# Strassen weight sums by accumulating DMA, and a third of K through Strassen, in a decoder trunk's shared K/V projection

## The chip, the cores and the metric

One Trainium2 chip, one core. The metric is the device time of one launch in microseconds (us), the median of several runs. TensorE is called PE here, VectorE DVE, ScalarE ACT, GpSimd POOL and SyncE SP, as the profile does.

## The reference

A two-layer decoder trunk on 256 tokens and 256 memory tokens of width 2048, in float32. Layer A is retention with a memory branch. After it, K and V for three groups of dilated attention are projected from the normalized residual stream; layer B uses them. The part that the change is about:

```python
def shared_kv(x, g, w_kv):
    B, S, _ = x.shape
    parts = split_cols(rmsnorm(x, g) @ w_kv, [DIL_W] * (2 * len(DIL_CONFIG)))
    return [t.reshape(B, S, DIL_HEADS, DIL_DH) for t in parts]
```

`w_kv` is 2048 x 12288: K1, V1, K2, V2, K3, V3 of 2048 columns each (K3 is called K's third group below). The memory's K and V of each layer are `rmsnorm(mem) @ w_mem_kv`.

## The kernel before

Every large product runs on PE in fp32r. A float32 operand is split into a high and a low part, and three of the four partial products are kept. A weight tile of 128 x 1024 floats (512 KB) comes from HBM into one of 6 buffers `raw`, on SP's queue. ACT casts it to `wh` (line 97), DVE computes `wl = raw - wh` (line 98). There are 5 pairs of `wh`/`wl`; `high_priority` lets these splits run ahead of PE, and a `raw` buffer is free when its last reader is done.

Two ways of multiplying matter here:

- `dense_cols` (line 306) computes a chunk of 512 columns, transposed: for each of 8 weight tiles, 8 pairs of a 512-column matmul (line 315, high part of the weight times high and low part of the input side by side) and a 256-column matmul (line 317): 64 pairs a chunk. K is made this way, 12 chunks. Its results have the columns on the partitions, which is what the attention wants of K.
- `strassen` (line 343) computes 1024 columns with 7 products of half-size blocks instead of 8, rows (tokens) on the partitions. One "pair" (of chunks) is 28 pieces, each ended by a `yield`: 4 steps d of four pieces (first phase: b0, b1, b2, b3), then 4 steps of three. A piece, which the text calls a product, is one split weight tile and 6 matmuls of 512 columns (lines 371 to 373). In the first phase a step loads w11, w12, w22 and needs three sums: s1 = w11 + w12, w12 + w22 (in place), s2 = s1 + w22 (line 361); in the second phase one load, w21, and s2 + w21. V is made this way, 6 pairs. The inputs of four of the products are differences of blocks of y, made by `combine`.

The generators of the Strassen pairs stand in the queue `woven`; `dense_cols` calls `weave(n)` to run n of their pieces after each of its weight tiles. Other small work stands in `pending`, one piece per `step()`. The framework's scheduler then fixes the order of each engine's queue; each queue runs strictly in that order. POOL's queue holds little else than the DMAs to and from DRAM: `spill` (line 778) puts a result into DRAM when it has been evicted from PSUM, `fetch` brings it back.

The order of stages: memory K and V of layer A, layer A, its output projection, memory K and V of layer B (`mk_b`, `mv_b`; meanwhile `make_y` turns and scales y), then the stage of K and V: a K chunk alone with `combine` beside it, 11 K chunks with six Strassen pairs woven in, 2 + 2 + 1 + 0 + 3 = 8 products per half of a chunk. After it layer B (`w_b`), and the output projection. At the very start, `dense_cols_first` fills the accumulators acc0 and acc1, and the next chunk (`mk1`, line 821) takes acc0 again.

The lines of the prediction's steps:

```python
            ahead(dve.tensor_tensor, s1, w11, w12, ALU.add)
            ahead(dve.tensor_tensor, w12, w12, w22, ALU.add)
            ahead(dve.tensor_tensor, s2, s1, w22, ALU.add)
```

Of the kernel before, what the change touches and what calls it, by code (L numbers as in the profile page):

```python
# [28 lines left out]
def yoco_trunk_kernel(  # L29
# [273 lines left out]
        for i in range(2):  # L303
            evict(i, ps[i])

    def dense_cols(xs, w, c, evict, g=None):
        for i in range(2):
            ps = acc_tile()
            for j in range(4):
                part = xs[j]  # L310
                for a, (wh, wl) in enumerate(weights(w[c, i, j], g, 4 * j, 4)):
                    first, last = j == 0 and a == 0, j == 3 and a == 3
                    for ct in range(2):
                        cs = slice(ct * P, (ct + 1) * P)
                        pe.matmul(ps[:, ct].rearrange("p h s -> p (h s)"), lhsT=wh[:, cs], rhs=xhl(part, a),  # L315
                                  start=first, stop=False, skip_group_check=True)
                        pe.matmul(ps[:, ct, 0, :], lhsT=wl[:, cs], rhs=xh(part, a),  # L317
                                  start=False, stop=last, skip_group_check=True)
                    if a % 2:
                        step()  # L320
                weave((2, 2, 1, 0)[j])
            if woven:
                with tc.high_priority(2 * AHEAD):
                    evict(i, ps)
                weave(3)
            else:
                evict(i, ps)

# [14 lines left out]
    def strassen(parts, comb, w, done, banks=[]):  # L343
# [35 lines left out]
        for d in range(4):  # L379
            w11, w12, w22 = (load(q, d) for q in range(3))  # L380
            s1, s2 = flat(big_tile()), flat(big_tile())
            ahead(dve.tensor_tensor, s1, w11, w12, ALU.add)
            ahead(dve.tensor_tensor, w12, w12, w22, ALU.add)
            ahead(dve.tensor_tensor, s2, s1, w22, ALU.add)
            keep.append(s2)
            f, l = d == 0, d == 3
            product(b0, w12, com(7), d, f, l)
            if l:
                with tc.high_priority(2 * AHEAD):
                    c7 = tmp.tile([P, 512], F32, name="p12")  # L390
                    act.copy(c7, b0)
            yield
            product(b1, s1, com(5), d, f, l)
            if l:
                with tc.high_priority(2 * AHEAD):
                    c5 = tmp.tile([P, 512], F32, name="p")
                    act.copy(c5, b1)
            yield
            product(b2, w22, com(3), d, f, l)
            yield  # L400
            product(b3, w11, own(0, 0), d, f, l)
            if l:
                with tc.high_priority(2 * AHEAD):
                    dve.tensor_tensor(c5, c5, b3, ALU.subtract)
                    dve.tensor_tensor(o1[:, 1, :], b3, c7, ALU.subtract)
                    dve.tensor_tensor(o2[:, 0, :], b2, c5, ALU.add)
                    dve.tensor_tensor(o2[:, 1, :], c7, c5, ALU.add)
            yield
# [79 lines left out]
        dense_cols(*job[:3], evict, *job[3:])  # L488
        return h, l

    def cols_scaled(b, *job):
        o = big_tile()

        def evict(i, ps):
            fold(half(o, i), ps)
            if b is not None:
                scale_half(o, i, b)

        dense_cols(*job[:3], evict, *job[3:])
        return o  # L500

    def scale_half(o, i, b):
# [315 lines left out]
    mk0 = big_tile()  # L818
    dense_cols_first(ms, memt, w_mk[0, 0:1], lambda i, ps: fold(half(mk0, i), ps))
    pending.append(stats_m())  # L820
    mk1 = cols_scaled(None, ms, w_mk[0], 1)
    drain()
    for i in range(2):
        scale_half(mk1, i, n_m.b)
# [50 lines left out]
        dve.memset(o, v)  # L875
        setattr(n_y, f, o)

    comb = {}

    def make_y():  # L880
        ss = small.tile([P, 2], F32, name="ss")
        dve.tensor_reduce(ss, part, AX.X, ALU.add)
        n_y.rstd(ss)
        yield
        for c in range(4):
            for t in range(2):
                act.activation(x1[c][:, t, :], x1[c][:, t, :], AF.Copy, scale=n_y.r[:, t:t + 1])
            yield
            yk.src[c] = yb.src[c] = big_tile()
            yield from turn_cols(x1[c], yk.src[c])  # L890
            yield from yk.start(c)

    pending.append(make_y())
    mk_b = [spill(flat(cols_scaled(n_m.b, ms2, w_mk[1], c))) for c in range(2)]
    mv_b = [spill(rows_scaled(dense(ms2, w_mv[1], c), n_m.r).rearrange("p t c -> p (t c)")) for c in range(2)]
    drain()
    kd, vd = {}, {}

    def done(p):
        def f(o1, o2):  # L900
            for n, o in ((2 * p, o1), (2 * p + 1, o2)):
                vd[n // 4, n % 4] = spill(o.rearrange("p t c -> p (t c)"))
        return f

    pending.append(combine(yk.raw, comb))
    for i in range(3):
        for hg in range(4):
            kd[i, hg] = spill(flat(cols_plain(yk, w_kc, 4 * i + hg)))
            if not kd.keys() - {(0, 0)}:
                drain()  # L910
                for p in range(6):
                    woven.append(strassen(yk, comb, w_vs[p], done(p)))
    while woven:
        weave()

# [11 lines left out]
        yield  # L927

    for j in range(4):
        pending.append(yb.start(j))  # L930
    mix = SplitMix()
    for c in range(2):
# [163 lines left out]
```

## Time and profile before

| | us |
|---|---|
| runs | 1897.88, 1902.39, 1902.02 (median 1902.02) |
| the profiled execution | 1899.93, its span 1898.2 |
| PE busy in the span | 1875.5 (99%) |
| DVE busy | 1317.7 (69%) |
| ACT busy | 985.8 (52%) |
| POOL busy | 47.5 (3%) |
| DMA | 385 MB, mean 203 GB/s |

The page gives busy time by engine, the same in 40 slices, and the chain of work that ended last. PE's matmuls overlap in the records, so a matmul's price is read from the distance of two starts, not from its duration. The trace is also asked for sums over stretches, for instructions in order of time, and for who waited for whom.

### The profile page before, as it was taken

The page shows a single profiled execution, that of the slowest core. Times are in us where ns is not written, and L with a number is a line of the kernel's source. Part 1 is how long each engine was busy: PE and PEld are TensorE (multiplying, and loading weights), DVE is VectorE, ACT ScalarE, POOL GpSimd, SP SyncE. Part 2 cuts the span into 40 slices and gives each one's busy share as a digit, 9 for nine tenths or more (in the row PEclk, how much of TensorE's full clock was granted, in tenths as well). Part 3 has the DMA queues.
Part 4 walks back from the last instruction along what each step waited for, and adds up shares of the span by engine and source line. Part 5 has one row for each costly group of instructions (what it writes and reads, how often), then busy time and mean ns, then how long its engine had stood idle before and what let it go on. Part 6 is the DMA issues. An engine that isn't in the chain of part 4 may idle for free.

```text
span 1898.2 us, 25963 instructions
## 1 busy us (share of the span) xinstructions
PE 1875.5 (99%) x9988; PEld 1604.6 (85%) x9988; DVE 1317.7 (69%) x1571; ACT 985.8 (52%) x1288; POOL 47.5 (3%) x88
## 2 busy tenths in 40 slices
PE   8999999999999999999999999999999999999997
PEld 7888888888888888888888888788889898888886
DVE  7766765665564757899999999866657475656643
ACT  6554445444454645555655556554545454545543
POOL 1000000000000000000000000000000000000000
PEclk9999999999999999999999999999999999999999
DMA  9654565565676666575766667666655556566462
GB/s 304 234 167 157 162 202 180 168 202 184 215 253 208 196 213 212 201 251 192 244 211 222 240 203 256 233 222 210 202 187 181 187 160 218 165 207 220 151 199 100
DMA packets 112588, 385.25 MB, mean 203 GB/s; under 512 B 12385, under 2 KB 18577, under 8 KB 112465
## 3 DMA queue, kind: packets, MB, share of 16 engines
q1 hardware_dynamic: 102784, 349.22, 56.5%
q0 software_dynamic: 9536, 34.37, 5.0%
q8 instruction: 78, 1.28, 0.3%
q14 instruction: 46, 0.37, 0.1%
q10 hardware_dynamic: 144, 0.01, 0.0%
HBM read 364.68 MB, written 18.87 MB: 202 GB/s over the span
## 4 chain that ended last, share of the span: by engine, by line
PE 93%; DVE 2%; issue 2%; ACT 1%; DMA 1%; SPq 0%; POOL 0%; ACTq 0%; POOLq 0%; DVEq 0%
PE acc L315 33%; PE acc L317 17%; PE acc L440 9%; PE acc L441 9%; PE acc L442 9%; PE acc L371 4%; PE acc L372 4%; PE acc L373 4%; DVE wl L98 1%; PE att L102 1%; PE att L103 1%; PE att L101 1%; PE acc L298 1%; ACT wh L97 1%; PE att L714 1%
## 5 line engine op out<-in xcount | busy, mean ns | idle before, releaser
L98 DVE TENSOR_TENSOR wl<-raw,wh 128x1024 fp32r<-128x1024 f32 (+1 forms) x642 | 769.3, 1209 | 461.8 <-ACT wh L97 459.9
L97 ACT CAST wh<-raw 128x1024 fp32r<-128x1024 f32 (+1 forms) x642 | 660.4, 1040 | 673.8 <-PE acc L315 263.6
L315 PE MATMUL acc<-big,wh 128*128 128x512 f32 x2752 | 983.5, 400 | 5.6 <-DVE big L221 2.4
L317 PE MATMUL acc<-big,wl 128*128 128x256 f32 x2752 | 771.3, 280 | 0.8 <-DVE wl L98 0.8
L315 PEld LDWEIGHTS acc<-big,wh 128*128 128x128 f32 x2752 | 517.8, 188 | 127.7 <-DVE big L470 3.1
L317 PEld LDWEIGHTS acc<-big,wl 128*128 128x128 f32 x2752 | 520.2, 189 | 5.0 <-DVE wl L98 1.1
L440 PE MATMUL acc<-wh,big 128*128 128x512 f32 x744 | 291.6, 392 | 0.0
L441 PE MATMUL acc<-wl,big 128*128 128x512 f32 x744 | 289.8, 390 | 0.0
L442 PE MATMUL acc<-wh,big 128*128 128x512 f32 x744 | 289.8, 390 | 0.0
L442 PEld LDWEIGHTS acc<-wh,big 128*128 128x128 f32 x744 | 139.7, 188 | 29.1
L440 PEld LDWEIGHTS acc<-wh,big 128*128 128x128 f32 x744 | 139.8, 188 | 28.2
L441 PEld LDWEIGHTS acc<-wl,big 128*128 128x128 f32 x744 | 139.8, 188 | 27.8
L371 PE MATMUL acc<-wh,big 128*128 128x512 f32 x336 | 133.2, 397 | 1.2 <-ACT wh L97 1.0
L372 PE MATMUL acc<-wl,big 128*128 128x512 f32 x336 | 131.7, 392 | 0.5 <-DVE wl L98 0.5
L373 PE MATMUL acc<-wh,big 128*128 128x512 f32 x336 | 131.6, 392 | 0.0
L97 ACT CAST wh<-big 128x1024 fp32r<-128x1024 f32 x72 | 75.5, 1049 | 72.5 <-DVE big L361 57.7
L98 DVE TENSOR_TENSOR wl<-big,wh 128x1024 fp32r<-128x1024 f32 x72 | 87.8, 1220 | 19.3 <-ACT wh L97 19.1
L371 PEld LDWEIGHTS acc<-wh,big 128*128 128x128 f32 x336 | 63.1, 188 | 17.1 <-ACT wh L97 1.7
L373 PEld LDWEIGHTS acc<-wh,big 128*128 128x128 f32 x336 | 63.1, 188 | 14.8
L372 PEld LDWEIGHTS acc<-wl,big 128*128 128x128 f32 x336 | 63.2, 188 | 11.8 <-DVE wl L98 1.0
L361 DVE TENSOR_TENSOR big<-big,raw 128x1024 f32<-128x1024 f32 x48 | 58.5, 1219 | 0.3
L98 DVE TENSOR_TENSOR big<-big 128x512 fp32r<-128x512 f32 (+1 forms) x54 | 43.4, 823 | 4.6 <-ACT big L97 3.2
(230 smaller groups left out, 1264.5 us busy)
## 6 DMA issues: line engine op xcount, KB each, us to landing
raw<-in_w_b_dram SPq DMA_DIRECT2D x160, 512.0 KB, 3.5
raw<-in_w_kc_dram SPq DMA_DIRECT2D x96, 512.0 KB, 4.4
raw<-in_w_vs_dram SPq DMA_DIRECT2D x96, 512.0 KB, 4.5
raw<-in_w_ac_dram SPq DMA_DIRECT2D x64, 512.0 KB, 3.5
raw<-in_w_ar_dram SPq DMA_DIRECT2D x64, 512.0 KB, 3.9
raw<-in_w_oa_dram SPq DMA_DIRECT2D x48, 512.0 KB, 3.5
raw<-in_w_ob_dram SPq DMA_DIRECT2D x48, 512.0 KB, 3.5
raw<-in_w_mv_dram SPq DMA_DIRECT2D x32, 512.0 KB, 3.5
```

What stands on the lines that cost most here:

```text
L97: act.copy(hi, src)
L98: dve.tensor_tensor(lo, src, hi.bitcast(F32), ALU.subtract)
L101: pe.matmul(o, lhsT=ah, rhs=bh, start=first, stop=False, skip_group_check=True)
L315: pe.matmul(ps[:, ct].rearrange("p h s -> p (h s)"), lhsT=wh[:, cs], rhs=xhl(part, a), start=first, stop=False, skip_group_check=True)
L317: pe.matmul(ps[:, ct, 0, :], lhsT=wl[:, cs], rhs=xh(part, a), start=False, stop=last, skip_group_check=True)
L361: f(*args)
L371: pe.matmul(ps, lhsT=h, rhs=wh[:, cs], start=first, stop=False, skip_group_check=True)
L372: pe.matmul(ps, lhsT=h, rhs=wl[:, cs], start=False, stop=False, skip_group_check=True)
L373: pe.matmul(ps, lhsT=l, rhs=wh[:, cs], start=False, stop=last, skip_group_check=True)
L440: pe.matmul(ps[t], lhsT=xh(part, a)[:, ts], rhs=wh, start=first, stop=False)
L441: pe.matmul(ps[t], lhsT=xh(part, a)[:, ts], rhs=wl, start=False, stop=False)
L442: pe.matmul(ps[t], lhsT=xl(part, a)[:, ts], rhs=wh, start=False, stop=last)
```

## The change

Five things. (1) In `strassen`, s1 is loaded from w11's DRAM by SP and w12 added to it by an accumulating DMA on POOL's queue; w12 gets w22 added in the same way. DVE keeps s2 = s1 + w22 and s2 + w21. (2) K's third group leaves the K chunks (8 instead of 12) and becomes two more Strassen pairs (8 instead of 6), whose results `turn_out` turns on PE, four 128 x 128 transposes to a PSUM bank, and spills. All pairs are queued before the first K chunk, and weaving is denser: 4 + 4 + 3 + 0 + 4 = 15 products per half chunk. (3) `combine` moves into the second chunk of memory V. (4) The turned y is spilled to DRAM and fetched again for layer B, instead of being kept in four `big` tiles. (5) `mk1` starts with the accumulator acc2.

```diff
-    def dense_cols(xs, w, c, evict, g=None):
+    def dense_cols(xs, w, c, evict, g=None, name=None):
         for i in range(2):
-            ps = acc_tile()
+            ps = acc_tile(name if i == 0 else None)
...
-                weave((2, 2, 1, 0)[j])
+                weave((4, 4, 3, 0)[j])
             if woven:
                 with tc.high_priority(2 * AHEAD):
                     evict(i, ps)
-                weave(3)
+                weave(4)
...
             s1, s2 = flat(big_tile()), flat(big_tile())
-            ahead(dve.tensor_tensor, s1, w11, w12, ALU.add)
-            ahead(dve.tensor_tensor, w12, w12, w22, ALU.add)
+            sp.dma_start(out=s1, in_=w[0, d])
+            pool.dma_start(out=s1, in_=w[1, d], accum_op=ALU.add)
+            pool.dma_start(out=w12, in_=w[2, d], accum_op=ALU.add)
             ahead(dve.tensor_tensor, s2, s1, w22, ALU.add)
...
-    mk1 = cols_scaled(None, ms, w_mk[0], 1)
+    mk1 = cols_scaled(None, ms, w_mk[0], 1, name="acc2")
...
-            yk.src[c] = yb.src[c] = big_tile()
+            yk.src[c] = big_tile()
             yield from turn_cols(x1[c], yk.src[c])
+            yd.append(spill(flat(yk.src[c])))
...
-    mv_b = [spill(rows_scaled(dense(ms2, w_mv[1], c), n_m.r).rearrange("p t c -> p (t c)")) for c in range(2)]
+    mv_b = []
+    for c in range(2):
+        if c == 1:
+            pending.append(combine(yk.raw, comb))
+        mv_b.append(spill(rows_scaled(dense(ms2, w_mv[1], c), n_m.r).rearrange("p t c -> p (t c)")))
     drain()
     kd, vd = {}, {}
+
+    def turn_out(o, key):
+        t = big_tile()
+        yield from turn_cols(o, t)
+        kd[key] = spill(flat(t))
...
-                vd[n // 4, n % 4] = spill(o.rearrange("p t c -> p (t c)"))
+                if n < 12:
+                    vd[n // 4, n % 4] = spill(o.rearrange("p t c -> p (t c)"))
+                else:
+                    pending.append(turn_out(o, (2, n % 4)))
...
-    pending.append(combine(yk.raw, comb))
-    for i in range(3):
+    for p in (0, 1, 6, 2, 3, 7, 4, 5):
+        woven.append(strassen(yk, comb, w_vs[p], done(p)))
+    for i in range(2):
         for hg in range(4):
             kd[i, hg] = spill(flat(cols_plain(yk, w_kc, 4 * i + hg)))
-            if not kd.keys() - {(0, 0)}:
-                drain()
-                for p in range(6):
-                    woven.append(strassen(yk, comb, w_vs[p], done(p)))
     while woven:
         weave()
...
     for j in range(4):
+        yb.src[j] = fetch(yd[j])
         pending.append(yb.start(j))
...
-        "w_kc": cblocks(cat(w_kv, (0, 2048), (4096, 6144), (8192, 10240))),
-        "w_vs": sblocks(cat(w_kv, (2048, 4096), (6144, 8192), (10240, 12288))),
+        "w_kc": cblocks(cat(w_kv, (0, 2048), (4096, 6144))),
+        "w_vs": sblocks(cat(w_kv, (2048, 4096), (6144, 8192), (10240, 12288), (8192, 10240))),
```

Three places of the queues of the changed kernel follow; the DMA rows of lines 383 and 384 are the accumulating ones (383 into s1, 384 into w12), 382 is s1's load, 356 the loads of w11, w12, w22 and w21, 263 a K weight tile, 782 a spill.

POOL's queue where the stage of K and V begins; `spill11` is the last memory V chunk, the first pair's steps d = 0 and 1 follow:

```order
L384 DMA raw_6218<-in_w_vs_dram 128x1024
L384 DMA raw_6292<-in_w_vs_dram 128x1024
L782 DMA spill11_6186<-big_6183 128x1024
L383 DMA big_6222<-in_w_vs_dram 128x1024
L383 DMA big_6296<-in_w_vs_dram 128x1024
```

Before, POOL had only the spill here; now s1's accumulation of the first step stands behind it. In PE's queue the last memory V matmul is followed by the first product and then 16 K matmuls; after these comes the product that reads s1.

POOL's queue where the second pair follows the first; `spill12` and `spill13` are the first pair's results, `spill14` a K chunk, `raw_6814` and `big_6818` w12 and s1 of the second pair's step d = 1:

```order
L384 DMA raw_6736<-in_w_vs_dram 128x1024
L782 DMA spill13_6730<-big_6215 128x1024
L782 DMA spill14_6766<-big_6188 128x1024
L782 DMA spill12_6728<-big_6214 128x1024
L384 DMA raw_6814<-in_w_vs_dram 128x1024
L383 DMA big_6818<-in_w_vs_dram 128x1024
```

The second pair's accumulations from step 1 on stand behind the spill that the first pair's last eviction releases.

SP's queue in steps d = 2 and 3 of the third pair; `big_7436` and `big_7510` are s1:

```order
L356 DMA raw_7430<-in_w_vs_dram 128x1024
L356 DMA raw_7432<-in_w_vs_dram 128x1024
L382 DMA big_7436<-in_w_vs_dram 128x1024
L356 DMA raw_7434<-in_w_vs_dram 128x1024
L263 DMA raw_7482<-in_w_kc_dram 128x1024
L356 DMA raw_7504<-in_w_vs_dram 128x1024
L356 DMA raw_7506<-in_w_vs_dram 128x1024
L356 DMA raw_7508<-in_w_vs_dram 128x1024
L382 DMA big_7510<-in_w_vs_dram 128x1024
```

s1's load is new in this queue. In step 2 it stands ahead of w22 (`raw_7434`), in step 3 behind it (`raw_7508`), and w22's load needs a free `raw` buffer.

## Rows read from the trace of the kernel before

**Rows 1.** The page: busy time by engine; DVE's tenths in 40 slices.

```profile
PE 1875.5 (99%) x9988; PEld 1604.6 (85%) x9988; DVE 1317.7 (69%) x1571; ACT 985.8 (52%) x1288; POOL 47.5 (3%) x88
...
DVE  7766765665564757899999999866657475656643
```

**Rows 2.** The page: the chain that ended last, by engine.

```profile
PE 93%; DVE 2%; issue 2%; ACT 1%; DMA 1%; SPq 0%; POOL 0%; ACTq 0%; POOLq 0%; DVEq 0%
```

**Rows 3.** Sums, stage of K and V: PE, PEld, DVE, ACT, POOL busy, clock, DMA.

```profile
720.00:1227.00 507.00, 504.89 (x2545) 423.81 (x2543) 470.19 (x453) 290.14 (x319) 12.79 (x24) 1.00 0.67 224
```

**Rows 4.** Timeline of PE: start, duration; first matmuls of three K chunks, stage's end.

```profile
719.97 0.39 PE L315 MATMUL acc<-big,wh 128*128 128x512 f32 x1
...
742.57 0.40 PE L315 MATMUL acc<-big,wh 128*128 128x512 f32 x1
...
787.26 0.39 PE L315 MATMUL acc<-big,wh 128*128 128x512 f32 x1
...
1226.58 0.28 PE L317 MATMUL acc<-big,wl 128*128 128x256 f32 x1
```

**Rows 5.** Timeline of PE: matmuls with idle time before them, and the releaser.

```profile
33.43 0.50 PE L315 MATMUL acc<-big,wh 128*128 128x512 f32 x1 [2.00 <-DVE big L470]
...
902.43 0.50 PE L371 MATMUL acc<-wh,big 128*128 128x512 f32 x1 [0.59 <-ACT wh L97]
...
993.58 0.50 PE L372 MATMUL acc<-wl,big 128*128 128x512 f32 x1 [0.55 <-DVE wl L98]
...
1227.92 0.50 PE L315 MATMUL acc<-big,wh 128*128 128x512 f32 x1 [1.06 <-ACT wh L97]
```

**Rows 6.** The page: groups of the weight splits and of one weight sum.

```profile
L98 DVE TENSOR_TENSOR wl<-raw,wh 128x1024 fp32r<-128x1024 f32 (+1 forms) x642 | 769.3, 1209 | 461.8 <-ACT wh L97 459.9
L97 ACT CAST wh<-raw 128x1024 fp32r<-128x1024 f32 (+1 forms) x642 | 660.4, 1040 | 673.8 <-PE acc L315 263.6
...
L361 DVE TENSOR_TENSOR big<-big,raw 128x1024 f32<-128x1024 f32 x48 | 58.5, 1219 | 0.3
```

**Rows 7.** Waits of SP's DMA queue in the stage: total us, times, longest.

```profile
SPq L263 <- DVE wl L98: 209.4, 87, 8.5
SPq L356 <- DVE wl L98: 201.0, 96, 8.4
```

**Rows 8.** DMA queues and issues from 720 to 1203: share of 16 engines; us to landing.

```profile
q1 hardware_dynamic: 26179, 95.36, 60.2%
q0 software_dynamic: 3168, 11.54, 6.1%
...
raw<-in_w_vs_dram SPq DMA_DIRECT2D x96, 512.0 KB, 4.5
...
spill<-big POOLq DMA_DIRECT2D x22, 512.0 KB, 5.1
```

**Rows 9.** POOL's 32 fetches of line 786, 512 KB each, from issue to landing.

```profile
DMA to landing us min/median/max: 3.5/5.0/10.0
```

**Rows 10.** The same for the four fetches between 1275 and 1310, issued singly.

```profile
DMA to landing us min/median/max: 3.5/4.2/4.5
```

**Rows 11.** Line 751's transposes: duration ns min, median, max; first and last start.

```profile
L751 PE MATMUL att<-ident,big x20: 270/272/273, 633.8 to 657.9; 128*128 128x128 f32 x20
```

**Rows 12.** Timeline of PE: four such transposes in a row.

```profile
641.73 0.60 PE L751 MATMUL acc<-ident,big 128*128 128x128 f32 x4
```

**Rows 13.** Timeline, ACT and POOL after the last memory V matmul.

```profile
721.13 1.26 ACT L513 ACTIVATE big<-acc,r_m 128x512 f32<-128x512 f32 x2
...
722.68 0.53 POOL L781 DMA_DIRECT2D spill<-big  x1 [21.23 <-ACT big L513]
```

**Rows 14.** Timeline, PE, ACT and POOL after the last product of a Strassen pair.

```profile
1219.29 0.39 PE L315 MATMUL acc<-big,wh 128*128 128x512 f32 x1
...
1219.49 0.59 ACT L427 COPY big<-acc 128x512 f32<-128x512 f32 x1 [1.51 <-PE acc L373]
...
1220.37 0.53 POOL L781 DMA_DIRECT2D spill<-big  x1 [4.49 <-ACT big L427]
```

More of the change, by code (lines that the diff above doesn't have):

```diff
@@ L489, in cols_plain2, with cols_scaled @@
         return h, l
-    def cols_scaled(b, *job):
+    def cols_scaled(b, *job, name=None):
         o = big_tile()
@@ L497, in evict @@
                 scale_half(o, i, b)
-        dense_cols(*job[:3], evict, *job[3:])
+        dense_cols(*job[:3], evict, *job[3:], name=name)
         return o
@@ L876, in yoco_trunk_kernel @@
         setattr(n_y, f, o)
-    comb = {}
+    comb, yd = {}, []
     def make_y():
```

## The prediction

> **What bounds the kernel now.** I read the page's busy times first. PE is busy for 99% of the span, and DVE shows nines in eight slices near the middle, where K and V are made [rows 1]. PE carries 93% of the chain that ended last [rows 2]. So PE's own work sets the time, and the question is what PE executes and where it would be made to wait. In the stage of K and V, 720 to 1227, PE runs at a granted clock of 1.00, its full 2.4 GHz, and DVE is busy for 470.2 of 507 us, 93% [rows 3]: there it is nearly a second bound.
>
> The price of PE's work comes from starts in the timeline [rows 4]. The first K chunk, with no product woven in, goes from 719.97 to 742.57: **22.60 us**. The next, with 16 products, goes to 787.26: 44.69, so a product costs 22.09 / 16 = **1.381 us**. The stage's last matmul starts at 1226.58, so it ends about 0.12 later and the stage takes 506.7. By the two prices, 12 chunks and 168 products are 271.2 + 232.0 = 503.2: 3.5 us are waits, some of which the rows show, for splits (0.59 and 0.55 [rows 5]).
>
> The loads: SP's queue waited over 400 us for DVE's splits [rows 7]. Each load waits until a split frees one of 6 buffers, then takes 4.5 us to land [rows 8]. The buffers, not the queue, hold the loads back.
>
> **The change on PE's path.** The sums are made against the profiled execution, 1899.93.
>
> - Four K chunks go: 4 x 22.60 = -90.4.
> - Two Strassen pairs come, 56 products: 56 x 1.381 = +77.3.
> - Their results are turned: 4 tiles x 8 = 32 transposes. One is recorded with 0.27, four in a row with 0.60, so that a further one adds 0.11 [rows 11, 12]: +3.5.
> - `mk1` with acc2 no longer waits for the eviction of acc0: -2.0 [rows 5].
> - The stage's 3.5 us of waits go if DVE gets looser. DVE has 24 more splits (56 less 32, 1.21 each, +29) and 32 fewer sums (96 before, 64 after, 1.22 each, -39) [rows 6], and `combine` leaves the stage; I take all of it: -3.5.
>
> Together **-15.1**. ACT has as many more casts of 1.04 [rows 6] in a stage where it is busy for 290 of 507 [rows 3]; that stays covered. Spilling and fetching y adds 8 DMAs; the fetches stand in POOL's queue during the last K chunk, which has few products left, and are hidden unless they land over 20 us late. The wait at the start of layer B (1.06 [rows 5]) stays as it is. `combine` in the memory V chunk runs beside PE's 96 matmuls; nothing waits for it before the stage.
>
> **The new waits.** Let L be the time from the issue of an accumulating DMA to its landing. The trace has none. The nearest row is a fetch, same queue, size and direction: 3.5 at least, median 5.0, 10.0 at most [rows 9]; the long ones were issued four in a row, and four issued singly have a median of 4.2 [rows 10]. An accumulation also reads its 512 KB destination. One 512 KB DMA takes 6.1% of 483 us / 22 = 1.34 us of all 16 engines (POOL's queue), SP's 60.2% x 483 / 182 = 1.60 [rows 8]; so a second read adds 0 to 1.3. I take **L = 4.6**, between the median of the single fetches and that of all. For the range: 3.5 to 10.
>
> 1. *Start of the stage, once.* s1 of the first step is accumulated behind the last memory V spill. That spill was issued at 722.68, 2.71 after PE had turned to the next work at 719.97 [rows 4, 13]; then 0.53 for its issue, L, and 1.05 for ACT's cast: L + 4.3. PE has one product and 16 K matmuls before it needs s1: 1.38 + 2.83 = 4.2. DVE's sum and its split follow, about 0.9 more: the wait is **L + 1.0** = 5.6.
> 2. *Each change of pair, 7 times.* Two accumulations of step d = 1 stand behind the spill of the former pair's result. After a last product that spill was issued 1.08 after PE's next slot (1220.37 - 1219.29) [rows 14]; + 0.53 + L + 1.05 = L + 2.7. PE has four products and one K weight tile before step 1: 5.52 + 2.83 = 8.35. Nothing is lost while **L < 5.7**.
> 3. *Step d = 3 of each pair.* s1's load stands in SP's queue behind w22's, which waits for the buffer that w12's split of step 2 frees. From that split to s1's: 0.3 issue, 4.5 landing [rows 8], 0.1, L, a sum and a split (2.3): L + 7.2. PE has five products and a K tile, 9.7. It is short by L - 2.5, less DVE's lead: 5.7 - L left over from 2, and some 1.35 gained in a step (8.35 on PE against 6 DVE operations at about 1.17, 7.0). Nothing is lost while **2L < 9.5**, L < 4.8.
>
> A late accumulation also stops what is queued behind its reader: DVE and ACT run in order, so K's splits wait too, and the `raw` buffers are freed later.
>
> At L = 4.6 only item 1 counts: +5.6. Sum: -15.1 + 5.6 = **-9.5**, 1890.4 for the profiled execution. It lies 2.1 below the median of the runs shown (1902.0), so I forecast **1892** for the median. A change under about 0.3% (5.7 us) can't be told from none here.
>
> **The rivals.**
>
> - *Accumulations land late and PE waits in every pair* (slower). If the second read counts in full and the stage's heavier traffic costs as much again, L is near 6.5. Then item 1 is 7.5, item 2 is 0.8 x 7 = 5.6, item 3 is 4.0 less 1.35, 2.65 x 8 = 21: 34 in all, +19, **1921**. It decides from L = 5.3: there the three items are 6.3 + 0 + 8.4, about what the change gives. For it: this stage's own spills have a median of 5.1 at a DMA share of 67% [rows 3, 8], and in an order fixed beforehand a wait is never filled with other work. Against it: SP's loads of the same stage land in 4.5, and in the second phase nothing depends on an accumulation, so DVE can get ahead again. The Trainium skill, in "Collectives: The Full Stack", section "The bandwidth ceiling: the fold count and why AG ≠ RS ≠ AR", says that a reducing transfer is half as fast as a copy because it reads two sources on the same ring. No run so far shows an accumulation; by that rule this rival is the likelier of the two, by the fetch rows the forecast is. Chance 0.30.
> - *The DMA engines become the bound* (slower). The stage has 249 plain DMAs (224 loads, 25 spills) and 64 accumulations, for 216 before. At 1.34 to 1.60 each, and accumulations at one to two such, that is 334 + 86 = 420 up to 398 + 205 = 603 us, against PE's 180.8 + 309.3 + 3.5 = 493.6 in the stage. The low end is hidden, the high end isn't; in the middle and a little above, 550, it is +56 over PE: **1943**. Against it: bursts in the first phase can be spread into the second, when half as much is loaded. Chance 0.08.
> - *The gain is eaten* (no change): L of 5.0 to 5.6, or waits at other places, such as the two turned pairs, where s1 of the next pair's step 1 stands behind the spill of a turned tile. 10 to 20 us of waits: **1897 to 1907**. Chance 0.15.
>
> **How the numbers follow.** The forecast has 0.47, all of it faster by over 0.3%. So faster 0.47, same 0.15, slower 0.38. The lower end: no wait at all, 1902.0 - 15.1 = 1886.9, less the 4 us by which the lowest run shown lies under the median: 1883. The upper end takes in most of the first rival's spread, up to L = 7.1 (8.1 + 9.8 + 26.0 - 15.1 = +29): 1932. Left out are the second rival and the tails.
>
> **What would show it.** Right: the stage of K and V takes 490 to 500 instead of 506.7; accumulations land in under 5; PE has one wait of 5 to 6 us at its start, for the cast of s1, and few others; L470's wait at 33 is gone; DVE's share of the stage stays near 92%. Wrong: PE idles before lines 371 and 372 by some us in each pair, released by ACT or DVE that themselves waited for an accumulating DMA (landing over 5.7), or a DMA share near 1.00 in the first phases with loads that land in 6 us and more.

## The result, and the profile after

**2093.7 us** (recorded median of four runs) against 1901.6. Three of the four lie at 2086.5 to 2094.9, median 2092.5; the fourth, of 5320 us at a granted clock of 1.00, can't be compared with them and is left out of the ratio: 1.100, 95% interval 1.097 to 1.104. The change makes the kernel 10% slower; the forecast was 1892, its upper end 1932.

The page of the changed kernel. Groups are busy us, mean ns | idle before them and its releaser.

```profile
span 2090.8 us, 25945 instructions
...
PE 1939.6 (93%) x9844; PEld 1624.2 (78%) x9844; DVE 1315.0 (63%) x1571; ACT 1010.3 (48%) x1318; POOL 107.3 (5%) x160
...
PE   9999999999999878878688878889999999999998
...
DVE  7766755755547556757567566677665656565753
...
PEclk9999999999999989989899898899999999999999
...
L371 PE MATMUL acc<-wh,big 128*128 128x512 f32 x448 | 197.6, 445 | 102.7 <-ACT wh L97 95.7
...
L372 PE MATMUL acc<-wl,big 128*128 128x512 f32 x448 | 197.0, 440 | 23.7 <-DVE wl L98 23.5
...
L361 DVE TENSOR_TENSOR big<-big,raw 128x1024 f32<-128x1024 f32 x64 | 78.0, 1223 | 88.8 <-DMA big<-in_w_vs_dram 73.7
```

All of it is lost in the stage of K and V. DVE's nines of before [rows 1] have become fives, sixes and sevens: DVE isn't the bound any more, it waits too. PE's losses stand before the first two matmuls of a product: 102.7 us, nearly all for ACT's cast, and 23.7 for DVE's split. DVE's sum s2 (L361) waited 73.7 us for s1; before, that group waited 0.3 [rows 6].

The sums of the changed kernel's stage, from its first matmul to the first of layer B, in the form of [rows 3]. The last product ends at 1408.7, but the last half K chunk, 11 us, comes behind it:

```profile
716.69:1420.02 703.33, 570.02 (x2402) 444.41 (x2401) 460.91 (x439) 312.46 (x341) 69.61 (x90) 0.88 0.78 234
```

703 us for 507. By the prediction's prices PE has 180.8 + 309.3 + 3.5 = 493.6 of work here. It was idle for 703.3 - 570.0 = **133 us**; the remaining 570.0 - 493.6 = **76 us** is in the main the same work at a lower clock: the granted clock is 0.88 on average, and its two levels are 2.4 and 1.2 GHz, so about a quarter of the stage (0.12 x 2), some 165 us, passed at the lower one. (How the 76 us divide between the clock and waits too short to be seen as idle isn't resolved.) The DMA engines are at 0.78, not full.

One of these waits, in step d = 1 of the sixth pair, from the timelines of the changed kernel's POOL, ACT, DVE, SP and PE (start, us, instruction, idle before it):

```profile
1158.44 0.89 POOL L384 DMA_DIRECT2D raw<-in_w_vs_dram  x1 [1.79 <-DMA raw<-in_w_vs_dram]
...
1155.69 1.05 ACT L97 CAST wh<-raw 128x1024 fp32r<-128x1024 f32 x1
1167.73 1.04 ACT L97 CAST wh<-raw 128x1024 fp32r<-128x1024 f32 x1 [10.99 <-DMA raw<-in_w_vs_dram]
...
1159.10 1.22 DVE L361 TENSOR_TENSOR big<-big,raw 128x1024 f32<-128x1024 f32 x1 [1.11 <-DMA raw<-in_w_vs_dram]
1168.80 1.23 DVE L98 TENSOR_TENSOR wl<-raw,wh 128x1024 fp32r<-128x1024 f32 x1 [8.47 <-ACT wh L97]
...
1158.44 0.43 SPq L382 DMA_DIRECT2D big<-in_w_vs_dram  x1
1170.06 0.33 SPq L356 DMA_DIRECT2D raw<-in_w_vs_dram  x1
...
1162.84 0.39 PE L372 MATMUL acc<-wl,big 128*128 128x512 f32 x1
1163.07 0.40 PE L373 MATMUL acc<-wh,big 128*128 128x512 f32 x1
1168.82 0.80 PE L371 MATMUL acc<-wh,big 128*128 128x512 f32 x1 [5.36 <-ACT wh L97]
1170.08 0.80 PE L372 MATMUL acc<-wl,big 128*128 128x512 f32 x1 [0.46 <-DVE wl L98]
1170.67 0.63 PE L373 MATMUL acc<-wh,big 128*128 128x512 f32 x1
1171.10 0.63 PE L371 MATMUL acc<-wh,big 128*128 128x512 f32 x1
```

POOL can issue w12's accumulation only when w12's own load has landed (1158.44). It lands at 1167.7, over 9 us after its issue. Until then ACT stands at the cast of w12 and DVE at its split; K's splits, queued behind, don't run, and SP issues no load from 1158.9 to 1170.1. PE uses up what is split, idles 5.36 us, and then starts matmuls every 0.43 us where it had started them every 0.23: the clock has dropped.

The accumulations by themselves, from the views of lines 384 (w12) and 383 (s1) of the changed kernel:

```profile
L384 POOL DMA_DIRECT2D raw<-in_w_vs_dram x32: 863/872/1238, 702.5 to 1356.6; - x32
...
  DMA raw<-in_w_vs_dram: 113.3, 15
...
  ACT wh L97: 136.2, 22
...
DMA to landing us min/median/max: 5.3/8.1/11.4
...
L383 POOL DMA_DIRECT2D big<-in_w_vs_dram x32: 857/868/892, 719.0 to 1359.0; - x32
...
  DMA big<-in_w_vs_dram: 195.3, 26
...
DMA to landing us min/median/max: 5.5/8.1/14.0
```

They land in **8.1**, never under 5.3, where the prediction took 4.6. And POOL stood 195.3 us, 26 times of 32, waiting for s1's *first* transfer.

### The profile page after: what moved, and what is told of

Read it like the earlier page. It is cut to its first block, busy times and chain, and to the rows that moved or that the text cites. A ratio compares the mean times of both kernels' runs of the same rounds, so it can differ in the third digit from the quotient of the medians.

```text
span 2090.8 us, 25945 instructions
## 1 busy us (share of the span) xinstructions
PE 1939.6 (93%) x9844; PEld 1624.2 (78%) x9844; DVE 1315.0 (63%) x1571; ACT 1010.3 (48%) x1318; POOL 107.3 (5%) x160
## 5 line engine op out<-in xcount | busy, mean ns | idle before, releaser
L315 PE MATMUL acc<-big,wh 128*128 128x512 f32 x2496 | 901.1, 403 | 9.3 <-ACT wh L97 4.7
L317 PE MATMUL acc<-big,wl 128*128 128x256 f32 x2496 | 701.8, 281 | 1.1 <-DVE wl L98 1.1
L315 PEld LDWEIGHTS acc<-big,wh 128*128 128x128 f32 x2496 | 474.1, 190 | 125.3 <-ACT wh L97 11.4
L317 PEld LDWEIGHTS acc<-big,wl 128*128 128x128 f32 x2496 | 475.8, 191 | 5.6 <-DVE wl L98 2.1
L371 PE MATMUL acc<-wh,big 128*128 128x512 f32 x448 | 197.6, 445 | 102.7 <-ACT wh L97 95.7
L441 PE MATMUL acc<-wh,big 128*128 128x512 f32 x744 | 291.7, 392 | 0.0
L443 PE MATMUL acc<-wh,big 128*128 128x512 f32 x744 | 290.0, 390 | 0.0
L442 PE MATMUL acc<-wl,big 128*128 128x512 f32 x744 | 289.8, 389 | 0.0
L372 PE MATMUL acc<-wl,big 128*128 128x512 f32 x448 | 197.0, 440 | 23.7 <-DVE wl L98 23.5
L371 PEld LDWEIGHTS acc<-wh,big 128*128 128x128 f32 x448 | 93.4, 209 | 142.6 <-ACT wh L97 113.9
L97 ACT CAST wh<-big 128x1024 fp32r<-128x1024 f32 x96 | 100.6, 1048 | 197.0 <-DVE big L361 101.0
L373 PE MATMUL acc<-wh,big 128*128 128x512 f32 x448 | 191.6, 428 | 0.0
L443 PEld LDWEIGHTS acc<-wh,big 128*128 128x128 f32 x744 | 139.7, 188 | 29.1
L441 PEld LDWEIGHTS acc<-wh,big 128*128 128x128 f32 x744 | 139.8, 188 | 28.1
L442 PEld LDWEIGHTS acc<-wl,big 128*128 128x128 f32 x744 | 139.8, 188 | 27.7
L372 PEld LDWEIGHTS acc<-wl,big 128*128 128x128 f32 x448 | 93.6, 209 | 56.1 <-DVE wl L98 37.1
L361 DVE TENSOR_TENSOR big<-big,raw 128x1024 f32<-128x1024 f32 x64 | 78.0, 1223 | 88.8 <-DMA big<-in_w_vs_dram 73.7
L98 DVE TENSOR_TENSOR wl<-big,wh 128x1024 fp32r<-128x1024 f32 x96 | 117.2, 1221 | 25.8 <-ACT wh L97 25.8
L373 PEld LDWEIGHTS acc<-wh,big 128*128 128x128 f32 x448 | 94.2, 210 | 19.2
```

The costliest lines, as they stand in the source:

```text
L97: act.copy(hi, src)
L98: dve.tensor_tensor(lo, src, hi.bitcast(F32), ALU.subtract)
L361: f(*args)
L371: pe.matmul(ps, lhsT=h, rhs=wh[:, cs], start=first, stop=False, skip_group_check=True)
L372: pe.matmul(ps, lhsT=h, rhs=wl[:, cs], start=False, stop=False, skip_group_check=True)
L373: pe.matmul(ps, lhsT=l, rhs=wh[:, cs], start=False, stop=last, skip_group_check=True)
```

## The experiments

The prediction missed, so 17 kernels ran. "Before" took 1899 to 1902 beside each. Except where more are named, a time is one run; kernels that ran several times spread by 4 to 10 us, so single runs that lie closer than about 10 us are not told apart. The expectations of the first runs name theories by letters of their own; the text after each says what fell.

**1. Both sums back on DVE, all else as changed**

```diff
-            sp.dma_start(out=s1, in_=w[0, d])
-            pool.dma_start(out=s1, in_=w[1, d], accum_op=ALU.add)
-            pool.dma_start(out=w12, in_=w[2, d], accum_op=ALU.add)
+            ahead(dve.tensor_tensor, s1, w11, w12, ALU.add)
+            ahead(dve.tensor_tensor, w12, w12, w22, ALU.add)
```

> The change with s1 and w12 + w22 summed by DVE again; eight pairs, K's third group and the dense weaving stay. Theory A (the accumulations land late, 8.1 us, and their readers wait): the accumulation waits go, DVE becomes the bound: its 450 us of the stage plus 64 sums of 1.22 = 528 us, at a share of 95% a stage of about 555, total 1950 to 1970. Theory B (the stage's DMA traffic is too much): the traffic falls with the 96 extra transfers, so the same, 1950 to 1970. Theory C (15 products per half chunk leave the six raw buffers no room, whoever adds): 2050 or more.

Measured 1957.8: 136 of the 192 us go with the accumulating DMAs, 56 stay with the rest of the change (eight pairs in eight K chunks). DVE is busy there for 521 of 560 us.

**2. The DMA sums alone, in the kernel before** (six pairs, old weave)

```diff
-            ahead(dve.tensor_tensor, s1, w11, w12, ALU.add)
-            ahead(dve.tensor_tensor, w12, w12, w22, ALU.add)
+            sp.dma_start(out=s1, in_=w[0, d])
+            pool.dma_start(out=s1, in_=w[1, d], accum_op=ALU.add)
+            pool.dma_start(out=w12, in_=w[2, d], accum_op=ALU.add)
```

> The kernel before with only the accumulating DMAs for s1 and w12 (six pairs, 8 products per half chunk as before). Theory A: each of six pairs loses what each of eight loses in the change, about 20 to 25 us, so 2010 to 2050. Theory B: less traffic per us than in the change (six pairs over the same stage), 1900 to 1960. Theory C: as before, 1890 to 1905.

Measured 2034.0: +132 us with nothing else changed. The denser weave isn't needed for the harm.

**3. Plain transfers in the place of the accumulating ones** (the two additions are left out)

```diff
-            pool.dma_start(out=s1, in_=w[1, d], accum_op=ALU.add)
-            pool.dma_start(out=w12, in_=w[2, d], accum_op=ALU.add)
+            pool.dma_start(out=s1, in_=w[1, d])
+            pool.dma_start(out=w12, in_=w[2, d])
```

> The change with the two accumulating DMAs replaced by plain DMAs from the same DRAM tile to the same buffer on the same queue: nothing is added, all waits and bytes from HBM stay; left out is the addition (and the reading of the destination). Theory A: the plain DMAs land in about 5 us as a fetch does, and the time falls to 1900 to 1950. Theory B: the HBM traffic is the same, so 2030 to 2090. Theory C: 2050 or more.

Measured 2034.3. The two lines' landings in this kernel, w12's first:

```profile
DMA to landing us min/median/max: 3.6/4.9/9.9
...
DMA to landing us min/median/max: 3.7/5.2/10.9
```

They land about as predicted, and 133 us of loss remain. So what the addition itself does to a transfer (its later landing, its longer issue, its second read) is 59 us of the 192; a second transfer that depends on the first does harm even when it is quick. POOL still waited 178.1 us for s1's first load.

**4. The small parts without the sums and the two pairs**: `mk1` with acc2, `combine` in the second memory V chunk, pairs woven from the first K chunk (11 runs).

```diff
-    mk1 = cols_scaled(None, ms, w_mk[0], 1)
+    mk1 = cols_scaled(None, ms, w_mk[0], 1, name="acc2")
...
+        if c == 1:
+            pending.append(combine(yk.raw, comb))
...
+    for p in range(6):
+        woven.append(strassen(yk, comb, w_vs[p], done(p)))
...
-            if not kd.keys() - {(0, 0)}:
-                drain()
-                for p in range(6):
-                    woven.append(strassen(yk, comb, w_vs[p], done(p)))
```

> The kernel before with acc2 for mk1, combine in the second memory V chunk, and the six pairs woven from the first K chunk on; no DMA sums, K's third group as before. All theories: -2.0 for acc2, the rest beside other work: 1896 to 1900, ratio 0.998 to 1.000.

Measured 1896.5 against 1899.5, ratio 0.998 (0.997 to 0.999): **0.2% faster than the kernel before**, about the size that the prediction gave to these parts (2.0 and some of 3.5).

**5. Both sums on GpSimd**

```diff
-            sp.dma_start(out=s1, in_=w[0, d])
-            pool.dma_start(out=s1, in_=w[1, d], accum_op=ALU.add)
-            pool.dma_start(out=w12, in_=w[2, d], accum_op=ALU.add)
+            ahead(pool.tensor_tensor, s1, w11, w12, ALU.add)
+            ahead(pool.tensor_tensor, w12, w12, w22, ALU.add)
```

> The change with s1 and w12 + w22 added by GpSimd (POOL) as an instruction on the landed tiles, no accumulating DMA and no extra load. The trace has no POOL addition of 128 x 1024; DVE's takes 1.22 us. If DVE's load alone had been the obstacle and a POOL addition takes under 4 us and disturbs nobody, the change's own sum comes true: 1890 to 1900. If POOL's additions are long (64 of them at 7.5 us fill the stage of 490 us) or hold DVE up, 1950 to 2100.

Measured 2021.5. From this kernel's groups by form, over the whole run for POOL and over the stage for DVE:

```profile
L361 POOL TENSOR_TENSOR raw<-raw 128x1024 f32<-128x1024 f32 x32 | 101.7, 3177 | 32.9 <-DMA raw<-in_w_vs_dram 26.8 <-DVE wl L98 4.7 <-POOL big L361 0.2
...
L98 DVE TENSOR_TENSOR wl<-raw,wh 128x1024 fp32r<-128x1024 f32 x187 | 288.7, 1572 | 17.8 <-ACT wh L97 17.5
```

POOL takes 3.2 us for what DVE does in 1.22, and DVE's splits go from 1.21 [rows 6] to 1.57 meanwhile: no way out.

**6. Spills issued by ACT's queue**

```diff
-        pool.dma_start(out=d, in_=t)
+        act.dma_start(out=d, in_=t)
```

> The change with the spills issued on ACT's queue; POOL's queue holds only the accumulations and the fetches. Theory D (accumulations stand behind spills that wait for evictions): 1990 to 2050. Theory A (the chain of two transfers one behind the other, 5.5 + 8.1 us, with w12 in one of six raw buffers all that time): 2070 to 2100. Theory B (traffic): as A.

Measured 2098.3: spills that wait in POOL's queue aren't what holds the late sums back here.

**7. Sums begun one step earlier** (in each pair; s1 and w12 in big tiles, their loads still on SP)

```diff
+        def sum_ahead(d):
+            if d < 4:
+                s1, w12 = flat(big_tile()), flat(big_tile())
+                sp.dma_start(out=w12, in_=w[1, d])
+                sp.dma_start(out=s1, in_=w[0, d])
+                pool.dma_start(out=w12, in_=w[2, d], accum_op=ALU.add)
+                pool.dma_start(out=s1, in_=w[1, d], accum_op=ALU.add)
+                sums[d] = s1, w12
...
```

> The change with w12 loaded into a big tile instead of one of the six raw buffers, and both sums' loads and accumulations written one step d ahead of their use. The transfers and bytes stay the same. Theory A: most waits inside a pair go, 1900 to 1970. Theory B: the traffic is the same, 2050 to 2100. Theory D: the spills still stand ahead in POOL's queue at each change of pair, 2000 to 2060.

Measured 2027.9: 66 us come back, far from all. Step 0 of a pair has no step ahead of it, but only 11 of the 94 us by which PE is still idle in the stage lie there. POOL waited 212 us for w12's first loads, which still stand in SP's queue behind loads that wait for a buffer.

**8. Eight load buffers**

```diff
-RAW = 6
-BIG = 30
+RAW = 8
+BIG = 28
```

> The change with 8 raw buffers instead of 6 (and 28 big tiles instead of 30). Theory A: loads start some 4 to 5 us earlier, half of the time by which the sums are late: 1980 to 2040. Theories B and D: 2070 to 2100.

Measured 2055.4, 38 us better: the buffers that the chain holds longer are a part, not the cause.

**9. No sums at all**

```diff
-            pool.dma_start(out=s1, in_=w[1, d], accum_op=ALU.add)
-            pool.dma_start(out=w12, in_=w[2, d], accum_op=ALU.add)
```

> The changed kernel without its 64 accumulating DMAs and with nothing in their place (left out: the additions w11+w12 and w12+w22; s1 is a plain load, w12 a plain load). Theory W (each sum is two transfers that depend on each other and begin when the step is already due; the engines' fixed orders stand still meanwhile): PE gets the change's -15.1 and nearly no waits, 1880 to 1900. Theory O (the denser weave and the order of splits on DVE and ACT cost by themselves, whatever makes the sums): 1930 or more. Theory T (traffic): half of the extra transfers are gone, so about half of the loss, 1970 to 2000.

Measured 1926.3, between W's and O's numbers: 167 us of the loss hang on the sums, but the rest of the change costs 26 against before, not -15. The sums of its stage:

```profile
715.08:1254.77 539.69, 512.39 (x2402) 414.87 (x2400) 460.81 (x440) 315.73 (x341) 14.97 (x28) 0.98 0.69 243
```

PE's busy time is 512.4 for the 493.6 of the prediction's prices; of the 19 us between, up to 11 are the clock of 0.98. New are 27 us of idling, in waits of up to 2.5 us. The longest, from the timelines of DVE and PE:

```profile
908.85 1.88 DVE L415 TENSOR_TENSOR big<-big,acc 128x512 f32<-128x512 f32 x3 [2.13 <-PE acc L373]
910.65 1.22 DVE L98 TENSOR_TENSOR wl<-big,wh 128x1024 fp32r<-128x1024 f32 x1
...
911.92 0.79 PE L372 MATMUL acc<-wl,big 128*128 128x512 f32 x1 [2.53 <-DVE wl L98]
```

This is the last step of a pair's second phase: DVE first waits for b0's last matmul and does the three operations that read b0 (line 415), and only then the split that PE's next product needs. Counted along PE's timeline (6 matmuls a product, 28 products a pair), 16 of the 27 us lie in this step, over the eight pairs; before, 1.4 over six. s1's first load, which this kernel still makes, is awaited by ACT for 28 us and by DVE for 24, but few of PE's waits go back to it (3 us).

**10. The same accumulations into two tiles that nobody reads**

```diff
...
+            for q in (1, 2):
+                pool.dma_start(out=aside[(2 * d + q) % len(aside)], in_=w[q, d], accum_op=ALU.add)
...
```

> The changed kernel with its 64 accumulating DMAs aimed at two tiles that nobody reads (left out: the additions w11+w12 and w12+w22): same transfers, same queues, but no product depends on an accumulation. Theory W (waiting on dependent transfers): 1880 to 1910. Theory T (the accumulations' traffic slows the loads or the engines' reads of memory): 1950 or more, with loads of w_vs that land in 5.5 or later. Theory O (order and density): 1930 or more, as without sums.

Measured 2023.4, but it doesn't say what was asked. From the timeline of PE:

```profile
722.01 0.47 PE L752 MATMUL acc<-ident,big 128*128 128x128 f32 x1 [91.63 <-ACT big L892]
```

With nothing to pace them, all 64 accumulations were issued between 531 and 782, ahead of the stage, which begins at 811; y's small instruction on POOL (line 184) stood behind them, and PE stood still 91.6 us before y was turned. Without that one idle time the span is 1929.7, that of no sums. Traffic within the stage was not tried by it. But it shows accumulations alone: from 684 to 716 nothing else ran, with a median landing of 5.4, and POOL's queue shows (packets, MB, share of 16 engines)

```profile
q0 software_dynamic: 1601, 5.84, 103.3%
```

5.84 MB are 11.1 tiles of 512 KB, and 1.033 x 32 / 11.1 = **2.97 us** of all 16 engines each: about twice the 1.34 to 1.60 of a plain transfer that the prediction read from [rows 8].

**11. s1 alone by DMA, w12 + w22 on DVE**

```diff
-            pool.dma_start(out=w12, in_=w[2, d], accum_op=ALU.add)
+            ahead(dve.tensor_tensor, w12, w12, w22, ALU.add)
```

> The changed kernel with s1 accumulated by DMA and w12 + w22 on DVE (32 sums of 1.22 us come back to DVE, 39 us). Theory W: one of two late sums is left in each step: between both on DVE (1957.8) and both by DMA (2093.7), 1970 to 2040. If one late sum is as bad as two, because PE waits once a step either way: 2050 to 2090. If w12's was the only one that mattered (its buffer is one of the 6): 1940 to 1965.

Measured 2058.5: one late sum keeps 101 of the 136 us that both cost (2058.5 less the 1957.8 of experiment 1), so two are far from twice as bad. That PE waits once a step either way is the expectation's reason; it fits, but no run tried it by itself.

**12. Both sums two steps ahead, across the pairs, first loads on POOL's queue**

```diff
+    def begin():
...
+            w = plan.pop(0)
+            s1, w12 = flat(big_tile()), flat(big_tile())
+            pool.dma_start(out=w12, in_=w[1])
+            pool.dma_start(out=s1, in_=w[0])
...
+    def make():
...
+            pool.dma_start(out=w12, in_=w[2], accum_op=ALU.add)
+            pool.dma_start(out=s1, in_=w[1], accum_op=ALU.add)
...
+            s1, w12 = sums()
```

(`sums` calls both and hands over what was made a step before.)

> The changed kernel with both sums' first loads on POOL's queue two steps ahead, across the pairs, into tiles of their own, and both accumulations one step ahead: as many transfers, as many accumulations, each needed some 8 us or more after its issue. Theory W: 1885 to 1930, better than DVE's own sums (1957.8). Theory T (traffic, or accumulations that slow everything): 2010 to 2090, as one step ahead gave 2027.9. Theory O: 1930 or more.

Measured 1953.7: **140 of the 167 us that hang on the sums come back with the same transfers and the same accumulations, begun earlier.** Begun earlier takes in three edits here: the order, the first loads in POOL's queue instead of SP's, and w12 in a big tile instead of a `raw` buffer; experiment 7, with the last one and one step of lead, gave 66, and what each is worth alone was not tried. W's number was still missed, by 24. The sums from the stage's start to its last product, and of 100 us at its start:

```profile
716.00:1272.00 556.00, 507.36 (x2343) 409.61 (x2342) 452.36 (x428) 313.48 (x336) 106.34 (x154) 0.96 0.92 291
...
720.00:820.00 100.00, 81.02 (x338) 63.55 (x337) 68.58 (x65) 47.51 (x51) 24.40 (x35) 0.86 1.01 305
```

Now the DMA engines are at 0.92 over the stage, 1.01 at its start, and loads of w_vs land in 7.2 (5.5 in the changed kernel, 4.5 before [rows 8]).

**13. No sums, eight load buffers** (the kernel of 9 with the edit of 8)

> The changed kernel without its accumulating DMAs (left out: the additions w11+w12 and w12+w22) and with 8 load buffers instead of 6 (big tiles 28 instead of 30). Without sums and with 6 it took 1926.3. Theory B (what is left there is loads that come late because six buffers hold them back): 1885 to 1905. Theory O (what is left is the order: DVE and ACT have 86% and 58% of the stage and their splits stand in a fixed order behind s1's, an eviction or each other): 1918 to 1930, no change.

Measured 1924.8: no change. The 26 us that the change costs without sums aren't a shortage of buffers; theory O stands, and the waits shown in 9 bear it out.

**14. Sums two steps ahead, six pairs, old weave, with the small parts of 4** (4 runs; `begin` and `make` as in 12)

> The kernel with the small parts only (K's three groups plain, six pairs, 1896.5), and w11+w12 and w12+w22 by accumulating DMA with first loads two steps and accumulations one step before they are used, across the pairs. The same sums begun when due cost 132 us (2034.0 against 1901.6). Theory W (lateness is the cost): 1890 to 1902, as DVE gets 58 us of slack and the transfers fit (6 pairs give 72 more over 507 us). Theory T (traffic, accumulations as such): 1930 or more, DMA share near 1.00 in the stage.

Measured 1943.9, ratio 1.024 (1.022 to 1.026): 90 us better than the same sums begun when due (2034.0; 3 of them are the small parts), but W's 1890 to 1902 fell. From the timelines of POOL and DVE, a spill and what waited for it:

```profile
764.03 0.56 POOL L780 DMA_DIRECT2D spill<-big  x1 [2.23 <-DVE big L469]
...
777.39 0.69 DVE L405 TENSOR_TENSOR big<-acc,p 128x512 f32<-128x512 f32 x1 [9.94 <-DMA spill<-big]
```

The spill stands behind four accumulations in POOL's queue and lands after 13 us; DVE waits 9.94 for the big tile that it held, and PE idled 9.1.

**15. The same with more big tiles**

```diff
-RAW = 6
-BIG = 30
+RAW = 4
+BIG = 32
```

> The kernel with six pairs, old weave and sums two steps ahead (1943.9) with 32 big tiles instead of 30 and 4 load buffers instead of 6. In its trace DVE waited 38 us for the landing of spills whose big tile it was to write again. Theory S (big tiles run out, as the sums hold up to eight): those waits go and the time falls to 1905 to 1925, unless four load buffers are too few. Theory T (traffic: loads land in 7 instead of 4.5): 1940 or more, since fewer load buffers hide a late landing less.

Measured 1975.4: worse. DVE's waits for spills do go, as theory S had it, but ACT's waits for w_kc's loads go from 38.5 us to 153.5. With loads that land in 6.4, four buffers are too few.

**16. The same as 14 with spills on ACT's queue** (the diff of 6)

> The same kernel (1943.9) with the spills issued from ACT's queue instead of POOL's, where they stand behind four accumulating transfers. Theory Q (a spill lands late, 13.3 us at 764.03, since POOL's transfers are worked off in order): spills land in about 5, DVE's waits for them go, 1905 to 1925. Theory T (traffic on all queues): no change within 10 us of 1944.

Measured 1917.6: 26 us better, within Q's numbers for the time. In the stage the longest landing of a spill falls from 16.6 to 10.9 and DVE's waits for spills from 38 us to 17, though the median hardly moves (7.0 to 6.5, where Q had 5). What didn't help against lateness (6) helps here, where the sums are early. Left are 21 us over the small parts alone, in a stage with a DMA share of 0.88 where w_kc's loads land in 6.8 (4.5 there), and ACT waited 39.9 us for them.

**17. The whole change, with both repairs** (12 and 6)

> The whole change with sums two steps ahead (1953.7) and the spills on ACT's queue. If lateness and the spills' place behind accumulations are most of what the sums cost, it comes near the changed kernel without any sums (1926.3): 1925 to 1940. If traffic is what is left (DMA share 1.01 in its first 200 us): 1943 to 1955, no change.

Measured 1948.7: traffic's number. Its first 100 us:

```profile
720.00:820.00 100.00, 88.80 (x406) 70.40 (x405) 78.08 (x73) 52.03 (x56) 18.80 (x26) 0.98 1.03 314
```

The 5 us below experiment 12 are within the spread. With the lateness gone the DMA engines are at 1.03 here, and the change ends 22 us above its own time without sums.

## Why the prediction was wrong, point by point

**PE's work: right within 4%.** -90.4 + 77.3 + 3.5 gives 493.6 in the stage; experiment 9 has 512.4 busy us, up to 11 of them the clock, and in an undisturbed row of products matmuls start every 0.23 us as before (1162.84 to 1163.07). `mk1` no longer waits at 33: no matmul there has idle time before it. From layer B's first matmul on, the two kernels take the same time (670 us).

**"I take all of it: -3.5" failed, by some 46 us.** That is the stage of experiment 9 against the forecast's work, 539.7 less 493.6, without any sum. DVE did get looser (461 of 540 us, 93% before [rows 3]), but PE idled 27 us where it had idled 2. A mean share under 90% doesn't make such waits go; they come from which instruction stands ahead. 16 of the 27 us lie in the pairs' last step, where the operations of line 415 stand ahead of a split (9). Why such waits were hidden before and aren't with the denser weave is argued: up to four products now follow each other where it was two or three, with fewer K matmuls between b0's last product and the next one. That more buffers don't help was shown (13).

**L = 4.6 failed: it is 8.1.** A fetch was the nearest row. The bound taken for the second read, 0 to 1.3 us, was worked out from the share of 16 engines; there it was nearly right (2.97 less 1.34 to 1.60, experiment 10), but the landing is longer by more: 5.4 with only accumulations running (10), and 8.1 in the stage, against 4.9 and 5.2 for a plain transfer at the same place, a factor of 1.6. The Trainium skill, in "Collectives: The Full Stack", section "The bandwidth ceiling: the fold count and why AG ≠ RS ≠ AR", says of collectives that a reducing transfer is half as fast as a copy. This case's rows agree with it in the time of the DMA engines (2.97 against 1.34 to 1.60) and give 1.6 in the landing. Experiment 3 puts the price of the addition at 59 us.

**Items 1 to 3 failed as a sum, whatever L is.** With L = 8.1 they give 9.1 + 2.4 x 7 + 4.25 x 8 = 60, so 45 over before: about 1947, not 2094. With the L of experiment 3, about 5, they give some 10, and 133 us are lost there. The formulas asked at one place at a time how late one accumulation is when all else is on time; for items 1 and 2 the thing ahead of it was a spill, and spills out of POOL's queue change nothing (6). What POOL waited for was s1's first load, 26 times of 32 and 195 us, so not in step 3 alone. Where PE's 133 us of idling lie, counted as in experiment 9:

| place | us | by the items, L = 8.1 |
|---|---|---|
| first step of the first pair (item 1) | 6 | 9 |
| step d = 1 (item 2) | 44 | 17 |
| step d = 2 | 24 | no item |
| step d = 3 (item 3) | 30 | 34 |
| last step of the second phase | 22 (16 without sums) | no item |
| elsewhere | 7 | no item |

Item 1's size, 6.1 for the forecast's 5.6, came out by luck: L was short by 3.5. The sentence that followed the items, that a late one also stops what is queued behind its reader and frees `raw` later, was right and got no price. The stop at 1158 shows it: ACT, DVE and then PE are held by one landing; while they stand, no split frees a buffer, SP issues no load, and the next step's chain of load, landing, issue, landing begins late as well. "DVE can get ahead again" in the second phase was the argument against it; it does, but for one step: step 0 of the seven later pairs has 1.4 us of waits in all, and step 1 is late again. What shows that lateness is the cost: begun two steps earlier, the same transfers cost 140 us less (12), 90 with the old weave (14), in both with the two other edits named at 12.

**The clock had no term.** Every wait was priced by its length. After 5.36 us without a matmul, matmuls started every 0.43 us instead of 0.23. PE's busy time in the stage is 570.0 with the sums and 512.4 without (9): 58 us, most of it the clock (0.88 against 0.98), beside 106 us more of idling.

**The rivals.** "Accumulations land late and PE waits in every pair" is what happened, with the rows named as the sign of it: PE idle before lines 371 and 372, released by ACT or DVE that waited for an accumulation. Its price, 1921, had the same faults. (The range's upper end, 1902.0 + 29, is 1931 and not 1932; that decides nothing.) "The DMA engines become the bound" was not this result (0.78), but it is what comes next: 1.01 to 1.03 in 100 us at the stage's start where the lateness is taken away (12, 17). Its 550 us of transfers were right: 0.78 x 703 = 549 in the changed kernel, 0.93 x 558 = 519 in 17. Both are more than the 507 us that the whole stage took before, so an order alone can hardly bring the change below the kernel before (an estimate; 1943 was this rival's price, 1953.7 and 1948.7 are measured).

**The account of the 192 us**: 26 without any sums (9, 13), 140 by late begin, with queue and buffer (changed kernel less 12), 27 left with a DMA share near 1 (12 less 9), of which moving the spills takes 5, within the spread (17). That the rest is traffic is argued from share and landings; no run took traffic alone away.

## What to carry to other kernels

Work that moves from an engine to a DMA gets a second landing in its chain: before you count the engine's time as saved, ask when the first transfer can be *issued*, and give the chain a lead of two landings and a buffer of its own. In a fixed order a wait isn't its own length: price also the instructions behind the waiting one on each engine, the buffers that aren't freed, and TensorE's lower clock afterwards. Try the small parts of a change alone: here they gain 0.2% and the large ones lose 10%.

## What the runs showed of the hardware that was not expected

- A 512 KB accumulating DMA lands in 8.1 us (median; 5.3 to 14.0) against 4.9 to 5.2 for a plain one at the same place, and in 5.4 with only such transfers running (experiment 10); its issue takes POOL 0.87 us (0.53 for a spill [rows 13]).
- It takes 2.97 us of all 16 DMA engines (experiment 10), about twice the 1.34 to 1.60 of a plain one [rows 8].
- After 5.36 us of idling PE's matmuls started every 0.43 us; by the mean granted clock some 165 us of the changed stage passed at 1.2 GHz, none of it before [rows 3].
- In a stage in which GpSimd adds 64 tiles of 128x1024 (2.9 to 3.2 us each), DVE's splits of the same size take 1.57 us on average instead of 1.21 [rows 6] (experiment 5).
- A 512 KB spill behind four accumulations in the same queue landed after 13 us (experiment 14); from ACT's queue the longest took 10.9 (16).
